# One set of buffers and PSUM banks for out projection, gate-up and down

## The chip, the cores and the metric

The kernel runs on one core of a Trainium2 chip. The metric is the device time of one launch in microseconds (us). The engines are TensorE (PE in the profile; PEld is its weight load), VectorE (DVE), ScalarE (ACT), GpSimd (POOL) and SyncE (SP), which here issues nearly all transfers. TensorE's clock has two levels, 1.2 and 2.4 GHz; the profile tells the granted share of the full one.

## What is computed

One layer of a latent model on 2048 tokens of width 1024: three parallel head groups (attention, a gated scan, Fourier mixing), an output projection, and a gated feed-forward network with 2816 hidden columns. The change concerns what follows the head groups:

```python
y = jnp.concatenate([attn, hg, fn], axis=-1) @ w_out[l]
x_new = x + g1 * y
x_new = x_new + g2 * swiglu_ffn(modulate(x_new, norm2_g[l], sh2, sc2), w_gate_up[l], w_down[l])
...
def swiglu_ffn(h, w_gu, w_dn):
    gate, up = jnp.split(h @ w_gu, 2, axis=-1)
    return (jax.nn.silu(gate) * up) @ w_dn
...
return rms_norm(x, final_norm_g)
```

All is float32.

## The kernel before

**Products.** Every float32 matrix product is made of three fp32r matmuls (`mm3`, lines 83 to 85): each operand is split into a high part (`hi`, line 72 on POOL, line 74 on ScalarE) and the rest (`lo`, line 79 on VectorE), and low x low is left out. So each operand tile costs a load, a cast and a subtraction before TensorE can use it.

**Out projection** (`project`, `second_norm`, `token_sums`; four blocks of 512 tokens). `mixed(b)` loads eight 128x512 tiles of the mixer's output from memory (`mr`, line 1118) and splits them to `hh` and `hl`; that of block 0 stands ahead of the last attention group, and the scheduler draws its work in among it. `project(b)` loads four 128x1024 row tiles of x (line 1130) and runs `rows_by_cols`: for each of two halves of 512 columns, two groups of four 128-row pieces of `w_out`, 1 MB a load (line 1044), split as a whole 128x2048 tile to `wh` and `wl`; 48 matmuls a group into four PSUM accumulators. `add_gated` (lines 1078 and 1079) adds g1 * y to x. `second_norm(b)` takes the mean squares on ScalarE (line 1086), stores the new rows to `xnew` (line 1140), scales them on POOL to `xn` (lines 124, 125, 1142), transposes them on TensorE in eight groups of four (line 1148), and ScalarE applies gain and shift to `xo` (line 1150), which is stored to `x2d` (line 1151). After the blocks 1 and 3 `token_sums` (lines 1158 to 1162) reads x2d back, forms four sums on VectorE (`block_sums`, lines 99 to 102) and stores them to `t2d`.

**Gate-up.** A seven-product (Winograd) scheme over a 2 x 2 split of tokens, depth and columns: `s` is one half of the tokens, and 22 units `j` of 128 hidden columns for each `s` take 44 units of seven products of twelve matmuls, in the order 6, 1, 5, 7, 2, 3, 4 and in three accumulators x, y, z. `operand(s, n)` (line 1201) loads the four tiles of product n's token operand through the slots `xraw` (four of them) and splits them to `xh`, `xl`. `fetch_w` (line 1213) loads a unit's weights, `left_sums` forms their sums (lines 94 to 97), `parts` splits them to `wp`. ScalarE, VectorE and POOL evacuate the accumulators (lines 1248 to 1273) to `e`, `f`, stored to `hid`.

**Down.** For each block `hidden(b)` loads and splits 22 tiles of `hid`, `rows_by_cols` multiplies them by `w_down` in groups of 1 MB, and `final` (lines 1097 to 1110) adds, normalises and stores.

**Order.** The three phases have pools of their own in SBUF and PSUM, opened and closed one after another, so a phase's first tiles wait for the end of the phase before where they take its space. Each engine runs its queue in order. The queues' order comes from a scheduler that moves instructions within what the data and the slots of the pools allow; SP's queue holds the transfers, and one that waits for a slot holds all behind it.

Of the kernel before, what the change touches and what calls it, by code (L numbers as in the profile page):

```python
# [42 lines left out]
def tile_backbone(  # L43
# [46 lines left out]
    def block_sums(x, o, left):  # L90

        x11, x12, x21, x22 = x
        if left:
            dve.tensor_tensor(o[0], x21, x22, ALU.add)
            dve.tensor_tensor(o[1], o[0], x11, ALU.subtract)
            dve.tensor_tensor(o[2], x12, o[1], ALU.subtract)
            dve.tensor_tensor(x21, x11, x21, ALU.subtract)
        else:
            dve.tensor_tensor(o[0], x12, x11, ALU.subtract)
            dve.tensor_tensor(o[1], x22, o[0], ALU.subtract)  # L100
            dve.tensor_tensor(o[2], x22, x12, ALU.subtract)
            dve.tensor_tensor(o[3], x21, o[1], ALU.subtract)
# [930 lines left out]

    with ExitStack() as ph:
        b2 = ph.enter_context(tc.tile_pool(name="p5b2", bufs=2, reuse_waits="tile"))
        hp = ph.enter_context(tc.tile_pool(name="p5h", bufs=13, reuse_waits="tile"))
        psd = ph.enter_context(tc.tile_pool(name="p5psd", bufs=4, side="right", reuse_waits="tile", space=PSUM))

        def split_w(loads, n):
            raw = b2.tile([P, 2048], F32, tag="wr", name="wr")  # L1040
            h = b2.tile([P, 2048], F32R, tag="wh5", name="wh5")
            l = b2.tile([P, 2048], F32R, tag="wl5", name="wl5")
            for dst, src in loads(raw):
                sp.dma_start(dst, src)
            hi(pool, h[:, :n], raw[:, :n])
            lo(l[:, :n], raw[:, :n], h[:, :n])
            return h, l

        def hidden_pair():
            return (hp.tile([P, TB], F32R, tag="hh", name="hh"),  # L1050
                    hp.tile([P, TB], F32R, tag="hl", name="hl"))

        def rows_by_cols(ah, al, w, kts, evac):

            last = len(kts) - 1
            for n in range(2):
                acc = [psd.tile([P, 512], F32, tag="dn", name="dn") for _ in range(4)]
                for i0 in range(0, len(kts), 4):
                    ni = min(4, len(kts) - i0)

                    def loads(raw):
                        return [(raw[:, :ni * 512].rearrange("p (k n) -> p k n", k=ni),
                                 w[kts[i0] * P:(kts[i0] + ni) * P, n * 512:(n + 1) * 512]
                                 .rearrange("(k p) n -> p k n", p=P))]
                    wh, wl = split_w(loads, ni * 512)
                    for t in range(4):
                        ts = slice(t * P, (t + 1) * P)
                        for i in range(ni):
                            ks = slice(i * 512, (i + 1) * 512)
                            mm3(acc[t], ah[i0 + i][:, ts], al[i0 + i][:, ts], wh[:, ks], wl[:, ks],  # L1070
                                i0 + i == 0, i0 + i == last)
                for t in range(4):
                    evac(t, n, acc[t])

        def add_gated(xs, gb):
            def evac(t, n, acc):
                ns = slice(n * 512, (n + 1) * 512)
                dve.tensor_tensor(acc, acc, gb[:, ns], ALU.mult)
                dve.tensor_tensor(xs[t][:, ns], acc, xs[t][:, ns], ALU.add)
            return evac  # L1080

        def mean_squares(xs):
            sq = b2.tile([P, 4], F32, tag="sq5", name="sq5")
            for t in range(4):
                junk = b1.tile([P, D], mybir.dt.bfloat16, tag="junk5", name="junk5")
                act.activation(junk, xs[t], AF.Square, accum_out=sq[:, t:t + 1])
            return rstd(b2, sq, 4, 1.0 / D, "r5")

        def final(b, xs):
            add = add_gated(xs, g2b)  # L1090
            sq = b2.tile([P, 4, 2], F32, tag="sq5f", name="sq5f")
            rs = b2.tile([P, 4, 2], F32, tag="rs5f", name="rs5f")

            def evac(t, n, acc):
                add(t, n, acc)
                junk = b1.tile([P, D], mybir.dt.bfloat16, tag="junk5", name="junk5f")
                act.activation(junk[:, :512], xs[t][:, n * 512:(n + 1) * 512], AF.Square, accum_out=sq[:, t, n:n + 1])
                if n == 0:
                    pool.tensor_scalar(rs[:, t, 0:1], sq[:, t, 0:1], 1.0 / D, EPS, ALU.mult, ALU.add)
                    return  # L1100
                pool.tensor_scalar(rs[:, t, 1:2], sq[:, t, 1:2], 1.0 / D, rs[:, t, 0:1], ALU.mult, ALU.add)  # L1101
                pool.tensor_tensor(rs[:, t, 0:1], rs[:, t, 1:2], half[:, 0:1], ALU.pow)  # L1102
                for s in range(2):
                    ns = slice(s * 512, (s + 1) * 512)
                    if s == 0:
                        dve.scalar_tensor_tensor(xs[t][:, ns], xs[t][:, ns], rs[:, t, 0:1], fgb[:, ns], ALU.mult, ALU.mult)
                    else:
                        act.activation(xs[t][:, ns], xs[t][:, ns], AF.Identity, scale=rs[:, t, 0:1])  # L1108
                        pool.tensor_tensor(xs[t][:, ns], xs[t][:, ns], fgb[:, ns], ALU.mult)  # L1109
                    sp.dma_start(out[0, b * TB + t * P:b * TB + (t + 1) * P, ns], xs[t][:, ns])  # L1110
            return evac

        def mixed(b):

            mh, ml = [], []
            for k in range(KT):
                raw = b2.tile([P, TB], F32, tag="mr", name="mr")
                sp.dma_start(raw, mixt[b][k * P:(k + 1) * P, :])
                h, l = hidden_pair()
                hi(act, h, raw)  # L1120
                lo(l, raw, h)
                mh.append(h)
                ml.append(l)
            return mh, ml

        def project(b, m):
            xs = []
            for t in range(4):
                xt = b1.tile([P, D], F32, tag="xt5", bufs=8, name="xt5")
                sp.dma_start(xt, x[0, b * TB + t * P:b * TB + (t + 1) * P, :])  # L1130
                xs.append(xt)
            rows_by_cols(m[0], m[1], w_out[0], list(range(KT)), add_gated(xs, g1b))
            return xs

        def second_norm(b, xs):

            r = mean_squares(xs)
            xn = []
            for t in range(4):
                sp.dma_start(xnew[b][t * P:(t + 1) * P, :], xs[t])  # L1140
# [227 lines left out]
```

## Time and profile before

| | |
|---|---|
| median of 3 runs | 3398.04 us (3397.04 to 3400.17) |
| profiled execution | 3395.07 us |
| its span | 3393.1 us |
| mean granted clock | 0.972 |
| TensorE busy | 3171.0 us (93%) |
| VectorE, ScalarE, POOL busy | 62%, 29%, 28% |

In the profiled execution the out projection's first matmul starts at 1754.9 us, gate-up's first at 2027.87, down's first at 2898.27, and the last matmul at 3379.4. In the timeline and groups, a line reads: line, engine, operation, written tile <- read tiles, shape, count; [idle before <- what ended it].

### The profile page before, as it was taken

Reading aid. Unit: us, or ns where it says so; the run is one execution under the profiler, and the core shown is the slowest. Engines: PE = TensorE matmul, PEld = TensorE weight load, DVE = VectorE, ACT = ScalarE, POOL = GpSimd, SP = SyncE. Lnnn points to the kernel's source line nnn. Section 1 sums busy time; section 2 is a strip of 40 time slices with the busy share of each in tenths; the row PEclk is TensorE's granted clock in tenths of the full one; section 3 lists DMA queues with packets and bytes.
Section 4 is the critical chain, followed back from the end, with each engine's and each line's share of the span. In section 5 each row is a group of like instructions: output and inputs, shape, how many; then the busy total and the mean of one; then the engine's idle time right before and its main releaser. Section 6 shows DMA issues by size and latency. Waiting matters only on the chain. (4 is left out here: it accounts for less than half of the span.)

```text
span 3393.1 us, 45128 instructions
## 1 busy us (share of the span) xinstructions
PE 3171.0 (93%) x17034; PEld 2648.8 (78%) x17034; DVE 2100.7 (62%) x3087; ACT 975.4 (29%) x2036; POOL 961.3 (28%) x1061
## 2 busy tenths in 40 slices
PE   7999999999889999999999849999999999899998
PEld 5777777787678888888887637888878887688886
DVE  6675665657776676776565447666776664554443
ACT  3222231222335555555542212111221111221110
POOL 3443444425411111110013213333233332232332
PEclk8999999999899999999999969999999999899999
DMA  6523232242541121221047764222432322664542
GB/s 225 170 70 123 76 115 83 61 133 67 169 136 51 35 63 51 76 61 35 7 145 249 264 211 142 80 89 75 137 106 77 91 75 71 231 210 152 181 157 79
DMA packets 355149, 392.49 MB, mean 116 GB/s; under 512 B 46362, under 2 KB 236660, under 8 KB 353908
## 3 DMA queue, kind: packets, MB, share of 16 engines
q1 hardware_dynamic: 340292, 378.59, 35.3%
q10 hardware_dynamic: 13776, 8.92, 0.8%
q8 instruction: 135, 2.21, 0.3%
q0 software_dynamic: 864, 2.10, 0.2%
q14 instruction: 82, 0.67, 0.1%
HBM read 302.77 MB, written 86.77 MB: 115 GB/s over the span
## 5 line engine op out<-in xcount | busy, mean ns | idle before, releaser
L83 PE MATMUL dn<-wl,hh 128*128 128x512 f32 x960 | 377.5, 393 | 20.4 <-DVE wl L79 20.4
L85 PE MATMUL dn<-wh,hl 128*128 128x512 f32 x960 | 377.1, 393 | 0.0
L84 PE MATMUL dn<-wh,hh 128*128 128x512 f32 x960 | 376.6, 392 | 0.0
L890 DVE TENSOR_REDUCE mx<-sc 128x1 f32<-128x512 f32 (+1 forms) x320 | 202.0, 632 | 122.3 <-PE sc L888 121.5
L72 POOL TENSOR_SCALAR wh<-wr 128x2048 fp32r<-128x2048 f32 x64 | 119.5, 1868 | 482.4 <-PE dn L85 388.0
L83 PE MATMUL y<-xl,wp 128*128 128x512 f32 x528 | 207.2, 393 | 45.9 <-DVE xl L79 42.3
L79 DVE TENSOR_TENSOR wp<-wr,wp 128x512 fp32r<-128x512 f32 x176 | 167.8, 954 | 120.6 <-POOL wp L72 117.8
L79 DVE TENSOR_TENSOR ptl<-ptv,pth 128x512 fp32r<-128x512 f32 x288 | 196.4, 687 | 67.1 <-ACT pth L74 64.7
L74 ACT CAST pth<-ptv 128x512 fp32r<-128x512 f32 x288 | 169.6, 593 | 236.2 <-PE ptv L904 228.6
L79 DVE TENSOR_TENSOR wl<-wr,wh 128x2048 fp32r<-128x2048 f32 x64 | 139.4, 2178 | 151.2 <-POOL wh L72 147.3
L896 ACT ACTIVATE p<-sc,mx 128x512 f32<-128x512 f32 (+1 forms) x320 | 201.9, 649 | 91.7 <-DVE mx L893 87.8
L83 PEld LDWEIGHTS dn<-wl,hh 128*128 128x128 f32 x960 | 181.2, 189 | 59.9 <-issue 20.6
L72 POOL TENSOR_SCALAR wp<-wr 128x512 fp32r<-128x512 f32 x176 | 132.3, 752 | 290.3 <-PE x L85 167.0
L85 PEld LDWEIGHTS dn<-wh,hl 128*128 128x128 f32 x960 | 181.1, 189 | 39.1
L84 PEld LDWEIGHTS dn<-wh,hh 128*128 128x128 f32 x960 | 181.1, 189 | 38.6
L84 PE MATMUL y<-xh,wp 128*128 128x512 f32 x528 | 206.9, 392 | 0.0
L85 PE MATMUL y<-xh,wp 128*128 128x512 f32 x528 | 206.4, 392 | 0.0
L888 PE MATMUL sc<-kth,q 128*128 128x512 f32 (+1 forms) x640 | 194.8, 378 | 0.0
L85 PE MATMUL accf<-xh,wl 128*128 128x512 f32 x448 | 184.6, 412 | 10.2 <-DVE wl L79 10.2
L79 DVE TENSOR_TENSOR wl<-wraw,wh 128x1536 fp32r<-128x1536 f32 (+3 forms) x78 | 118.5, 1519 | 119.6 <-POOL wh L72 117.7
L888 PE MATMUL sc<-kp,q 128*128 128x512 f32 (+1 forms) x640 | 190.0, 373 | 0.0
L79 DVE TENSOR_TENSOR hl<-mr,hh 128x512 fp32r<-128x512 f32 x120 | 98.3, 831 | 140.7 <-ACT hh L74 136.4
(350 smaller groups left out, 8067.4 us busy)
## 6 DMA issues: line engine op xcount, KB each, us to landing
wr<-in_w_gate_up_dram SPq DMA_DIRECT2D x88, 512.0 KB, 5.1
wr<-in_w_down_dram SPq DMA_DIRECT2D x40, 1024.0 KB, 5.1
wraw<-in_w_in_dram SPq DMA_DIRECT2D x112, 256.0 KB, 3.8
mr<-hid SPq DMA_DIRECT2D x88, 256.0 KB, 3.3
xt<-in_x_dram SPq DMA_DIRECT2D x32, 512.0 KB, 6.2
wm<-in_w_mod_dram SPq DMA_DIRECT2D x64, 256.0 KB, 2.8
wr<-in_w_out_dram SPq DMA_DIRECT2D x16, 1024.0 KB, 6.4
hid<-f SPq DMA_DIRECT2D x44, 256.0 KB, 3.8
```

The costliest lines, as they stand in the source:

```text
L72: pool.tensor_scalar(dst, src, 1.0, 0.0, ALU.mult, ALU.add)
L74: act.copy(dst, src)
L79: (eng or dve).tensor_tensor(dst, src, h, ALU.subtract)
L83: pe.matmul(ps, ah, bl, start=first, stop=False, skip_group_check=more)
L84: pe.matmul(ps, ah, bh, start=False, stop=False, skip_group_check=more)
L85: pe.matmul(ps, al, bh, start=False, stop=last, skip_group_check=more)
L888: pe.matmul(s[:, :n], a[:, ts], bb[:, js], start=i == 0, stop=i == 4)
L890: dve.tensor_reduce(mx[:, j:j + 1], s[:, :n], AX.X, ALU.max)
L896: act.activation(u["p"][:, a:e], u["s"][i][:, :e - a], AF.Exp, bias=mx[:, 5:6], accum_out=mx[:, 6 + i:7 + i])
```

## The change

Out projection, gate-up and down get one set of pools. Raw weights, raw mixer tiles and raw token sums share two slots of 128x4x512 (`raw4`). Split weights of all phases are 128x2x512 tiles of `wp`, nine of them (POOL casts one 512-wide part, VectorE subtracts). Operand pairs sit in 28 slots (`h1` to `h7`, `l1` to `l7`, four each); x rows borrow pairs 4 and 5. PSUM is handed out by `bank` from two pools of four in turn. The `xraw` slots fall from four to two (three in down). Loads of x and stores of xnew are 512 columns wide (256 KB) and the row scaling is in place.

Order in the program: a group's weights are loaded and split one group ahead (`Groups.ahead`). The transposes of block b - 1 (`turn_rows`) stand between the two halves of `project(b)`; those of block 3 in gate-up's unit 0. The sums of the first token half are formed on POOL during blocks 2 and 3 (`early_sums`), three of four stored and the fourth split at once as operand 6; those of the second half on VectorE in units 2 to 5 of gate-up. Operands 1, 7, 5 and the first unit's weights are loaded in block 3; operands 2, 3, 4 in unit 0. Down's first weights and 12 hidden tiles are split in the last unit. The matmuls and transposes are as many as before.

```diff
+        wr = ph.enter_context(tc.tile_pool(name="p5w", bufs=2, reuse_waits="tile"))
+        wp = ph.enter_context(tc.tile_pool(name="p5p", bufs=9, reuse_waits="tile"))
+        xa = ph.enter_context(tc.tile_pool(name="p5xa", bufs=4, reuse_waits="tile"))
+        psa = ph.enter_context(tc.tile_pool(name="p5psa", bufs=4, side="right", reuse_waits="tile", space=PSUM))
...
+        def bank(name):
+            banks["n"] += 1
+            return (psa, psb)[(banks["n"] - 1) // 4 % 2].tile([P, TB], F32, tag="bank", name=name)
...
+        def raw4(name):
+            return wr.tile([P, 4, TB], F32, tag="wr", name=name)
+
+        def wparts(src):
+            w = wp.tile([P, 2, TB], F32R, tag="wp", name="wp")
+            hi(pool, w[:, 0, :], src)
+            lo(w[:, 1, :], src, w[:, 0, :])
+            return w
...
+            def ahead(self, i):
+                if i < len(self.specs) and i not in self.done:
+                    self.done.add(i)
+                    self.load(i)
+                    for k in range(4):
+                        self.split(i, k)
+                self.load(i + 1)
...
+        st = gs.enter_context(tc.tile_pool(name="p5s", bufs=2, reuse_waits="tile"))
...
+            for g in range(2):
+                i = b * 4 + c * 2 + g
+                if i + 1 < len(wo.specs):
+                    wo.ahead(i + 1)
+                else:
+                    first_unit(0, 5)
+                w = wo.parts.pop(i)
+                for t in range(4):
+                    rows(acc[t], t, m, w, 4 * g, 4, KT)
...
+        def token_sums(s, k, eng):
+
+            raw = raw4("xr")
+            for i in range(4):
+                sp.dma_start(raw[:, i, :], x2d[s][i][k * P:(k + 1) * P, :])
+            t = st.tile([P, 3, TB], F32, tag="ws", name="ts")
+            block_sums(eng, [raw[:, i, :] for i in range(4)], [t[:, 0, :], t[:, 1, :]], False)
+            return raw[:, 0, :], (t[:, 0, :], t[:, 1, :], raw[:, 1, :], raw[:, 2, :])
...
-                raw = st.tile([P, TB], F32, tag="xraw", bufs=4, name="xraw")
+                raw = st.tile([P, TB], F32, tag="xraw", name="xraw")
...
+        def early_sums(ks):
+            for k in ks:
+                b11, ts = token_sums(0, k, pool)
+                keep_sums(0, k, ts, (0, 2, 3))
+                xo.setdefault(6, []).append(split(6, "xo", ts[1]))
+
+        wo.ahead(0)
+        xs = load_rows(0)
+        for b in range(NB):
+            sq = st.tile([P, 2, 4], F32, tag="sq5", name="sq5")
+            project(b, 0, m, xs, sq)
+            if b > 0:
+                turn_rows(b - 1, before)
+            if b + 1 < NB:
+                nm = mixed(b + 1)
+                nx = load_rows(b + 1)
+                if b + 2 == NB:
+                    early_sums((0, 1))
+            else:
+                wo.ahead(len(wo.specs) - 1)
+                xo |= {n: operand(0, n) for n in (1, 7, 5)}
+                raws.extend([fetch_w(0), fetch_w(1)])
+                raws.append(left_sums(raws.pop(0)))
+            project(b, 1, m, xs, sq)
+            scale_rows(xs, sq)
+            if b + 2 == NB:
+                early_sums((2, 3))
...
+                if i == 0 and n == 7:
+                    turn_rows(NB - 1, before)
+                if i == 0 and n == 1:
+                    xo |= {q: operand(0, q) for q in (2, 3, 4)}
...
+                elif o < 3:
+                    more_hidden(4 * (o + 1))
+                    if o == 0:
+                        wd.load(0)
+                        wd.load(1)
+                    for k in ((0, 1), (2,), (3,))[o]:
+                        wd.split(0, k)
+                    wd.done.add(0)
+            if s == 0 and 2 <= j < 6:
+                b11, ts = token_sums(1, j - 2, dve)
+                keep_sums(1, j - 2, ts, range(4))
```

The order of the engines' queues, where it moves, at three places. ScalarE at the end of attention, before the change (`pth` and `rbc` belong to attention, `hh` is the cast of block 0's mixer tiles):

```order
L74 CAST pth<-ptv 128x512
L74 CAST hh<-mr 128x512 x2
L74 CAST pth<-ptv 128x512 x3
L923 COPY rbc<-ptrc 128x512
L74 CAST pth<-ptv 128x512 x2
L74 CAST hh<-mr 128x512 x2
```

The same place in the changed kernel, where `mxh` is the cast of the mixer tiles:

```order
L74 CAST pth<-ptv 128x512
L74 CAST mxh<-mr 128x512 x8
L74 CAST pth<-ptv 128x512 x3
L923 COPY rbc<-ptrc 128x512
L74 CAST pth<-ptv 128x512 x5
L937 COPY at<-ptvu 128x512
```

All eight casts of the mixer's tiles now stand in one piece, ahead of the last attention casts. The next place is POOL in the out projection from block 2 to block 3, before (`wh` are the high parts of w_out, `xn` the scaled rows of block 2):

```order
L72 TENSOR_SCALAR wh_18001<-wr 128x2048
L72 TENSOR_SCALAR wh_18055<-wr 128x2048
L124 TENSOR_SCALAR r5m<-sq_18164 128x4
L125 TENSOR_TENSOR r5r<-r5m,half 128x4
L1142 TENSOR_SCALAR xn_18178<-xt_17868,r5r 128x1024
```

And after (`ts` and `xr` are the token sums, `xs` the rows scaled in place, `ss` the mean squares of block 2):

```order
L72 TENSOR_SCALAR wp<-wr 128x512 x8
L99 TENSOR_TENSOR ts<-xr 128x512
L100 TENSOR_TENSOR ts<-xr,ts 128x512
L101 TENSOR_TENSOR xr<-xr 128x512
L102 TENSOR_TENSOR xr<-xr,ts 128x512
...
L124 TENSOR_SCALAR r5m<-ss_18308 128x4
L125 TENSOR_TENSOR r5r<-r5m,half 128x4
L1160 TENSOR_SCALAR xs<-xs,r5r 128x512 x5
L72 TENSOR_SCALAR wp<-wr 128x512 x4
```

Two sets of four sums, which VectorE did before, stand ahead of the scaling of block 2 and of the split of block 3's first weights. The third place is SP's queue there, after (`xr` are the loads for the sums, `t2d` their stores, `wr_18176` block 3's first piece of w_out):

```order
L1177 DMA xr_18126<-x2d03_96 128x512
L1177 DMA xr_18143<-x2d00_93 128x512
L1184 DMA t2d00_101<-ts_18131 128x512
L1177 DMA xr_18143<-x2d01_94 128x512
L1177 DMA xr_18143<-x2d02_95 128x512
L1184 DMA t2d02_103<-xr_18126 128x512
L1184 DMA t2d03_104<-xr_18126 128x512
L1177 DMA xr_18143<-x2d03_96 128x512
L1184 DMA t2d00_101<-ts_18148 128x512
L1152 DMA xnew2_91<-xs_17687 128x512
L1079 DMA wr_18176<-in_w_out_dram 128x4x512
```

The piece of w_out, before alone among the stores of the transposed rows, now comes behind the loads and stores of the sums, and takes one of the two slots that these use.

## Rows read from the trace of the kernel before

**Rows 1.** Stretches: length, busy time (instructions) by engine, clock, DMA share, GB/s.

```profile
1800.00:1850.00 50.00, 47.10 (x212) 37.76 (x211) 24.88 (x25) 13.53 (x22) 15.76 (x10) 0.97 0.71 235
1850.00:1900.00 50.00, 46.69 (x209) 37.26 (x208) 25.53 (x32) 13.21 (x22) 13.54 (x9) 0.97 0.83 288
...
2000.00:2050.00 50.00, 20.94 (x74) 15.19 (x75) 37.06 (x52) 11.91 (x20) 12.90 (x15) 0.67 0.79 252
2050.00:2450.00 400.00, 399.78 (x1763) 330.20 (x1762) 277.85 (x377) 75.26 (x126) 130.11 (x168) 1.00 0.32 96
...
2927.00:3380.00 453.00, 452.75 (x1998) 374.56 (x1996) 198.23 (x188) 73.15 (x141) 126.54 (x99) 1.00 0.47 156
```

**Rows 2.** TensorE's waits after 1750 us: total us, times, longest.

```profile
PE y L83 <- DVE xl L79: 42.3, 1, 42.3
PE pt L1148 <- POOL xn L1142: 20.1, 7, 8.2
...
PE dn L83 <- DVE wl L79: 20.2, 1, 20.2
PE y L83 <- DVE t L1262: 3.6, 1, 3.6
```

**Rows 3.** TensorE's paces: one stretch, then timeline rows (start, busy us).

```profile
1768.00:1804.00 36.00, 36.00 (x156) 29.02 (x155) 25.25 (x28) 9.19 (x16) 7.66 (x5) 1.00 0.85 301
...
2028.43 0.63 PE L84 MATMUL y<-xh,wp 128*128 128x512 f32 x1
2028.86 0.63 PE L85 MATMUL y<-xh,wp 128*128 128x512 f32 x1
...
1917.23 5.53 PE L1148 MATMUL pt<-ident,xn 128*128 128x128 f32 x25 [0.20 <-POOL xn L1142]
```

**Rows 4.** Groups: line, engine, operation, count | busy us, mean ns | idle before.

```profile
L83 PE MATMUL dn<-wl,hh 128*128 128x512 f32 x960 | 377.5, 393 | 20.4 <-DVE wl L79 20.4
...
L72 POOL TENSOR_SCALAR wp<-wr 128x512 fp32r<-128x512 f32 x176 | 132.3, 752 | 290.3 <-PE x L85 167.0 <-issue 79.7 <-PE z L85 39.5
...
L1256 POOL TENSOR_TENSOR e<-e,e 128x512 f32<-128x512 f32 x44 | 57.4, 1306 | 11.3 <-ACT e L1255 11.3
...
L1150 ACT ACTIVATE xo<-pt,mod2t,gain 128x512 f32<-128x512 f32 x32 | 23.3, 776 | 40.6 <-PE pt L1148 26.5 <-DMA x2d<-xo 13.9
```

**Rows 5.** Timeline: first matmul of the out projection, last one of down.

```profile
1754.93 0.40 PE L83 MATMUL dn<-wl,hh 128*128 128x512 f32 x1
...
3379.36 0.39 PE L85 MATMUL dn<-wh,hl 128*128 128x512 f32 x1
```

**Rows 6.** Timeline of ScalarE at the end of attention.

```profile
1742.14 1.17 ACT L74 CAST hh<-mr 128x512 fp32r<-128x512 f32 x2
```

**Rows 7.** Transfers: count, KB each, median us from issue to landing.

```profile
wr<-in_w_out_dram SPq DMA_DIRECT2D x16, 1024.0 KB, 6.4
...
x2d<-xo SPq DMA_DIRECT2D x32, 256.0 KB, 4.2
xr<-x2d SPq DMA_DIRECT2D x32, 256.0 KB, 4.6
t2d<-xs SPq DMA_DIRECT2D x32, 256.0 KB, 3.0
```

**Rows 8.** A stretch of 10 us in the out projection, columns as in rows 1.

```profile
1830.00:1840.00 10.00, 10.00 (x45) 8.05 (x44) 4.00 (x4) 0.00 (x0) 1.91 (x1) 1.00 1.00 371
```

**Rows 9.** Timeline of POOL and VectorE with splits side by side.

```profile
2000.11 1.04 POOL L72 TENSOR_SCALAR wp<-wr 128x512 fp32r<-128x512 f32 x1
...
2000.59 1.09 DVE L79 TENSOR_TENSOR wp<-ws,wp 128x512 fp32r<-128x512 f32 x1
```

**Rows 10.** The raw operand tiles: duration ns min/median/max; time to landing.

```profile
L74 ACT CAST xh<-xraw x56: 606/621/628, 1989.0 to 2472.4; 128x512 fp32r<-128x512 f32 x56
L79 DVE TENSOR_TENSOR xl<-xraw,xh x56: 674/684/1137, 2027.0 to 2474.2; 128x512 fp32r<-128x512 f32 x56
...
DMA to landing us min/median/max: 2.5/3.2/5.1
```

More of the change, by code (lines that the diff above doesn't have):

```diff
@@ L1053, in rows_by_cols @@
[L1053 to L1111, printed above, removed]
@@ L1113, in mixed @@
-        def mixed(b):
[L1115 to L1133, printed above, removed]
@@ new lines, in rows @@
+        def rows(acc, t, m, w, k0, nk, kts):
+            ts = slice(t * P, (t + 1) * P)
+            for i in range(nk):
+                mm3(acc, m[k0 + i][0][:, ts], m[k0 + i][1][:, ts], w[i][:, 0, :], w[i][:, 1, :], k0 + i == 0, k0 + i == kts - 1)
+        def mixed(b):
+            out = []
+            for n, k0 in zip((1, 7) if b % 2 == 0 else (2, 3), (0, 4)):
+                raw = raw4("mr")
+                sp.dma_start(raw, mixt[b][k0 * P:(k0 + 4) * P, :].rearrange("(k p) n -> p k n", p=P))
+                out += [split(n, "mx", raw[:, k, :]) for k in range(4)]
+            return out
@@ L1164, in tile_backbone @@
         m = mixed(0)
+        wo = Groups(w_out[0], [(n, k0, 4) for _ in range(NB) for n in range(2) for k0 in (0, 4)])
         tasks = []
@@ new lines, in tile_backbone, with more_hidden @@
+        blocks6 = raws.pop()
+        DG = [(k0, min(4, HT - k0)) for k0 in range(0, HT, 4)]
+        wd = Groups(w_down[0], [(n, k0, nk) for _ in range(NB) for n in range(2) for k0, nk in DG])
+        hidden = []
+        stage = {}
+        def more_hidden(upto):
+            while len(hidden) < min(upto, NB * HT):
+                i = len(hidden)
+                raw = stage["p"].tile([P, TB], F32, tag="xraw", name="hr")
+                sp.dma_start(raw, hid[i // HT][i % HT * P:(i % HT + 1) * P, :])
+                hidden.append(split(ORDER[i // 4 % 7], "hd", raw))
@@ L1248, in tile_backbone @@
                     act.copy(e6, acc)
-                    if i + 1 < len(units):
+                    if not end:
                         blocks6 = left_sums(raws.pop(0))
@@ new lines, in tile_backbone @@
+                if not end:
+                    nxt[n] = wparts(blocks6[n])
+                elif o < 3:
[9 more added lines that the diff above has]
+                keep_sums(1, j - 2, ts, range(4))
```

250 lines of the change are left out of this document (133 added, 117 removed).

## The prediction

> **What bounds the kernel now.** I read the table of stretches first [rows 1]. From 2050 to 2450 us and from 2927 to 3380 us TensorE is busy all the time, at full granted clock: gate-up and down stand at TensorE's own pace, and no better order can gain there. The 50 us stretches of the out projection and of the step into gate-up are another picture: TensorE is busy for 47 of 50 us in two of them and for 20.94 in the last, at a granted clock of 0.67. The list of TensorE's waits names what ended these gaps [rows 2]: 42.3 us for the first operand of gate-up, 20.1 us in seven waits of the second norm's transposes for POOL's scaling, 20.2 us for down's first weights, 3.6 us where the operands are exchanged between the two token halves. That is 86.2 us.
>
> How much is lost in all? Two paces say it. In down, 1998 matmuls take 452.75 us, 0.2266 us each [rows 1]; in an undisturbed piece of the out projection 156 take 36 us, 0.231 us [rows 3]. After a gap the clock is at its lower level and a matmul starts every 0.43 us [rows 3] (its second and third row). The work is 960 x 3 = 2880 matmuls in the two projections [rows 4] and 44 units of 84 in gate-up, 6576 together: 1490 us at 0.2266. 768 of them belong to the out projection, + 3 us. The 128 transposes cost about 0.1 us each (an estimate: a run of 25 took 5.53 us at a lowered clock, the last of [rows 3]), 13 us. Sum 1506 us. From 1754.9, where the out projection's first matmul stands, to the last at 3379.6 [rows 5] the trace has 1624.7 us, an estimated 4 us of it for the last attention matmuls. **The loss is about 114 us**: 86 us of gaps, the rest slow clock after them and shorter waits. This is all that the change can win; it removes no matmul.
>
> **The change, part by part.** It does not take the causes of the gaps away, it puts their work earlier, beside TensorE's work. Each of the old gaps goes: the first unit's operands and weights are split during the last half of the out projection, the transposes of a block stand between the halves of the next, and down's first weights and 12 hidden splits stand in the last gate-up unit. So I strike the 114 us and ask what is late next, term by term, along the order of the changed kernel.
>
> *End of attention.* ScalarE now has eight mixer splits ahead of the last attention casts, before two; VectorE has their eight second halves and the first weight splits. Two casts take 1.17 us [rows 6], so six more cost 3.5 us on ScalarE, and VectorE about as much again in the same chain. I take 6 us, from 3 (VectorE's share hidden) to 9 (the weight splits in front too).
>
> *Join of blocks 2 and 3.* Let T be the start of the second half of block 2. The last transposed tile of the first token half leaves ScalarE 8 x 0.776 = 6 us later [rows 4] and lands after 4.2 us [rows 7], T + 11 with the queue; the load for the sums takes 4.6 us (T + 16); four sums on POOL at 1.306 us take 5.2 (T + 21) [rows 4]; their store takes 3.0 (T + 24). Only then is the shared raw slot free for block 3's first w_out load, which takes 6.4 us (T + 31), and its first split, 0.752 us on POOL [rows 4] and some 1.09 on VectorE [rows 9], makes T + 33. TensorE's 96 matmuls of the half end at T + 22 to 24. So it waits about 10 us, and 2 more for the clock. The order has the load behind the sums on SP's queue, and four more sums stand ahead of the row scaling on POOL. DMA is nearly full there: block traffic drove its share to 1.00 at 371 GB/s in one stretch of 10 us [rows 8]. I take 15 us, from 4 (the scheduler's loads land sooner) to 24 (every transfer at half speed).
>
> What VectorE and POOL do to each other is in [rows 9]: of two splits side by side POOL's takes 1.04 us and VectorE's 1.09, more than POOL's mean of 0.752 [rows 4] and VectorE's median of 0.684 [rows 10]. So each stretches the other, and the chain above has VectorE's stretched value. The Trainium skill ("SBUF — State Buffer", section "SBUF: two separate sides") says that a VectorE operation with two SBUF inputs and a GpSimd operation that reads SBUF lock the shared port pair, and the loser waits for the whole instruction. By that each of the four sums on the chain could wait a further 0.68 us, + 2.7 us, and the forecast would be 3337. The trace agrees only in part: its pair shows both engines busy from 2000.59 to 2001.15.
>
> *Unit 0.* The scale of block 3 stands behind ScalarE's evacuations, and three operands are loaded inside the unit: 6 us, from 1 to 15.
>
> *Exchange of the operands between the token halves.* The raw slots fall from four to two. A load takes 3.2 us, the cast 0.62, VectorE's part 0.68 [rows 10], with about 0.4 to issue: 4.9 us for a slot, with two slots 2.45 for each of 28 splits, 68.6 us. In the changed order 249 matmuls stand between the first and the last of them, 56.4 us. So 12 us are uncovered; before, with four slots, 3.6. I take 13 us with the clock, from 6 (loads at their minimum of 2.5 us) to 25 (at 5.1 for half of them).
>
> *Waits at the transposes.* They now stand between matmuls that are ready, so 1.5 us, from 0 to 5.
>
> *The rest*: the second w_out load of block 3, the start of down, the gate sums. Down's hidden splits are ready about 10, 20 and 32 us after the last unit's first product and needed at 19, 30 and 41, so that start is covered; if that cover fails, the 20.2 us of before come back. The chain behind the last matmul is the same code. 8 us, from 3 to 12.
>
> *At nothing*: splitting w_out in four parts of 512 columns takes POOL 0.752 x 4 = 3 us for a group [rows 4] and VectorE 4 x 1.09 at most; the 48 matmuls of a group, 11 us, cover both, and TensorE would pay what goes beyond 11. Smaller x and xnew transfers are twice as many on SP's queue; a half block's 6.3 million bytes take 17 us at the rate of [rows 8], beside 22 us of matmuls, and what they cost without that cover is B's price below.
>
> Sum of new losses: 6 + 15 + 6 + 13 + 1.5 + 8 = 49.5 us. Gain 114 - 49.5 = 64.5 us. The profiled execution took 3395.07 us; the median of the three runs is 3398.04, 3 us above it. 3398.0 - 64.5 = **3334 us** (rounded). The ends of the terms sum to 17 and 90, which would be 3301 and 3374, but they will not all fall one way.
>
> **The rivals.** *A: as above*, 3315 to 3350, chance 0.50.
>
> *B: the out projection becomes a DMA stage.* Each block moves w_out 4 MB, mixer 2, x 2, xnew 2, transposed rows 2, 12.6 million bytes; with the sums (7.3), the operands (3.1) and two gate weights the new order packs 63 MB into about 206 us, 306 GB/s, which no 50 us stretch of before reached: its four full stretches of the out projection moved 261.5 on average, from 235 to 288 [rows 1]. At that mean 63 MB take 241 us, 35 more: **3369 us**. Against it: at share 1.00 the engines moved 371 GB/s [rows 8], so the mean of before is what its gaps asked for, not a limit. Chance 0.22. The Trainium skill ("DMA: Bandwidth & Descriptors", section "Specifications") gives a core about 358 GB/s of HBM; by it 63 MB want 176 us, which is under 206. The trace's 371 is slightly above that figure.
>
> *C: the joins are covered.* If the loads at the join land before they are wanted and the exchange hides behind its 56 us, only the smaller terms stay, about 20 us: 3398 - 94 = **3304 us**. For it: two transfers that land in 3 us take most of the join's wait away. Against it: the join's chain above adds up with no slack. Chance 0.16.
>
> *D, slower: two raw slots act as one.* If the next load goes out only when the split before it is through, a split costs c = 4.9 us instead of 2.45. The 28 splits of the exchange and 22 of the first operands have 56 + 63 us of TensorE work beside them, so the loss is 50c - 119, with 30 us for the other terms. It eats the whole 114 us at c = 4.06; at 4.9 the loss is 156 us, 42 us slower: **3440 us**. For it: every such load waits on SP's one queue, where a wait holds all that follows. Against it: with four slots the exchange left only 3.6 us uncovered [rows 2], which a chain of 28 x 4.9 = 137 us could not have done. Chance 0.07.
>
> *E: nothing changes.* The order may be all that moves, with the clock's loss kept at the new joins; between C, B and D, 3391 to 3405. Chance 0.05.
>
> **How the numbers follow.** Faster and slower are counted beyond 0.2% (7 us), about what a measurement of this kernel can tell from no change. Faster: A, C and nearly all of B, 0.87. Same: E and the top of B, 0.05. Slower: D and a part of B joined to a late down start, 0.08. The range has to leave out 0.2: D, E and the top of B (0.14) above, and the part of C below 3298 (0.05). That gives 3298 to 3382 around 3334.
>
> **What would show it.** Right: no wait of TensorE above 5 us between the last attention matmul and block 2; one wait near the join of blocks 2 and 3, about 10 us, for a weight part; no 42 us gap before gate-up and no 20 us gap before down; granted clock over 0.9 in each 50 us stretch of the out projection; some 10 us around the exchange, ended by operand splits. The step on the join is wrong if the wait before block 3's first half is under 4 us; the step on the slots if 28 splits follow each other at 1.3 us. B is shown by a DMA share of 0.95 or more through two blocks with waits for transfers at each of them; D by operand loads that each start after the split before; the prediction as a whole is wrong if a wait over 25 us stands anywhere, above all at down's start.

## The result, and the profile after

The changed kernel takes **3349.06 us** (median of 4 runs, 3348.41 to 3351.47) against 3397.54 us for the kernel before on the same chip: a ratio of 0.9861, 95% interval 0.9849 to 0.9873. It is 1.4% faster. The forecast was 3334 us: the direction holds, the size was 15 us too good. In the profiled executions the span goes from 3393.1 to 3346.7 us.

TensorE's waits after 1735 us, in the changed kernel (what waited <- what ended it: total us, times, longest):

```profile
PE pt L1167 <- POOL xs L1160: 14.6, 4, 10.2
PE pt L1167 <- DVE xs L1149: 10.0, 6, 2.3
PE z L83 <- DVE xol L79: 9.2, 9, 1.6
PE ptv L904 <- DVE ptl L79: 7.3, 3, 4.0
PE y L83 <- DVE xol L79: 2.1, 4, 0.8
```

Set against [rows 2]: the 42.3 us before gate-up and the 20.2 us before down are gone. What is left are short waits, and the largest is one of 10.2 us. The stretches that hold them (length, busy time and instructions by engine, granted clock, DMA share, GB/s, as in [rows 1]):

```profile
1829.70:1840.30 10.60, 5.47 (x35) 4.49 (x34) 7.29 (x12) 6.51 (x14) 0.20 (x1) 0.75 0.48 165
...
1894.20:1917.30 23.10, 23.09 (x98) 18.67 (x96) 9.04 (x13) 9.20 (x19) 5.29 (x4) 0.95 0.92 319
1917.30:1957.50 40.20, 29.27 (x128) 23.48 (x128) 18.59 (x22) 9.39 (x19) 33.09 (x34) 0.83 0.77 254
1980.10:2050.00 69.90, 60.27 (x243) 46.11 (x243) 54.18 (x75) 26.39 (x45) 31.11 (x36) 0.90 0.56 172
2425.00:2480.00 55.00, 47.34 (x182) 34.30 (x181) 38.55 (x55) 17.73 (x30) 14.11 (x17) 0.94 0.56 165
...
2850.00:2900.00 50.00, 50.00 (x223) 41.40 (x222) 27.82 (x42) 15.17 (x25) 13.03 (x19) 1.00 0.70 237
```

The first is the transposes of block 0, the second and third the second half of block 2 and the join behind it, then gate-up's first units, the exchange of the operands, and the step into down, whose first matmul stands at 2854.43: TensorE works through it without a gap. The loss of a stretch is its length less its matmuls at 0.2266 us and its transposes at 0.1 us (a row's count holds one more, which reaches in over its start): 10.6 - 2 x 0.2266 - 3.2 = 6.9 us for the first; 69.9 - 210 x 0.2266 - 3.2 = 19 us for gate-up's start; 55 - 181 x 0.2266 = 14 us for the exchange.

### The profile page after: what moved, and what is told of

It is laid out like the page before. It is cut to its first block, busy times and chain, and to the rows that moved or that the text cites. A ratio compares the mean times of both kernels' runs of the same rounds, so it can differ in the third digit from the quotient of the medians.

```text
span 3346.7 us, 45666 instructions
## 1 busy us (share of the span) xinstructions
PE 3172.7 (95%) x17034; PEld 2653.5 (79%) x17034; DVE 2154.6 (64%) x3251; ACT 974.6 (29%) x2068; POOL 1057.7 (32%) x1269
## 5 line engine op out<-in xcount | busy, mean ns | idle before, releaser
L84 PE MATMUL dn<-wp,hdh 128*128 128x512 f32 x704 | 273.9, 389 | 0.0
L83 PE MATMUL dn<-wp,hdh 128*128 128x512 f32 x704 | 273.9, 389 | 0.0
L85 PE MATMUL dn<-wp,hdl 128*128 128x512 f32 x704 | 273.9, 389 | 0.0
L79 DVE TENSOR_TENSOR wp<-wg,wp 128x512 fp32r<-128x512 f32 x176 | 172.3, 979 | 100.4 <-POOL wp L72 97.9
L83 PE MATMUL y<-xol,wp 128*128 128x512 f32 x528 | 207.5, 394 | 2.3 <-DVE xol L79 2.1
L72 POOL TENSOR_SCALAR wp<-wg 128x512 fp32r<-128x512 f32 x176 | 125.5, 713 | 258.3 <-PE x L85 134.3
L84 PE MATMUL y<-xoh,wp 128*128 128x512 f32 x528 | 206.7, 391 | 0.0
L85 PE MATMUL y<-xoh,wp 128*128 128x512 f32 x528 | 206.3, 392 | 0.0
L72 POOL TENSOR_SCALAR wp<-ws 128x512 fp32r<-128x512 f32 x132 | 100.2, 759 | 296.8 <-PE y L85 158.8
L904 PE MATMUL ptv<-ident,p 128*128 128x128 f32 x1152 | 180.1, 276 | 9.1 <-DVE ptl L79 7.7
L83 PE MATMUL accf<-xl,wh 128*128 128x512 f32 x448 | 183.3, 409 | 0.0
L84 PE MATMUL accf<-xh,wh 128*128 128x512 f32 x448 | 182.1, 407 | 0.0
```

The lines of the kernel that those rows point to most:

```text
L72: pool.tensor_scalar(dst, src, 1.0, 0.0, ALU.mult, ALU.add)
L79: (eng or dve).tensor_tensor(dst, src, h, ALU.subtract)
L83: pe.matmul(ps, ah, bl, start=first, stop=False, skip_group_check=more)
L84: pe.matmul(ps, ah, bh, start=False, stop=False, skip_group_check=more)
L85: pe.matmul(ps, al, bh, start=False, stop=last, skip_group_check=more)
L904: pe.transpose(pt[:, i, u * P:(u + 1) * P], ps[u]["p"][:, (2 * g + i) * P:(2 * g + i + 1) * P], ident)
```

## The experiments

Each is an edit of the changed kernel unless it says otherwise. Ratios are to the kernel before, which ran beside each; a difference to the changed kernel is the difference of the ratios times 3397.5 us, and with intervals of about 0.0015 either way one of less than some 7 us is not clear of the noise. Then the trace alone speaks. For that the last column takes the profiled execution: the time from the first matmul behind attention's last one to the last matmul of down, against 1565.3 us in the changed kernel. It leaves out the head groups, whose instructions the runs have in common and whose end varies from 1762.7 to 1770.2 us.

| | median us | ratio (95% interval) | against the changed kernel | the same in the trace, behind attention |
|---|---|---|---|---|
| e1_banks | 3346.57 | 0.9855 (0.984 to 0.987) | -2 us | -1.6 us |
| e2_slots1 | 3425.3 | 1.0086 (1.0071 to 1.0101) | +76 us | +79.9 us |
| e3_slots3 | 3335.5 | 0.9824 (0.9809 to 0.9839) | -13 us | -8.6 us |
| e4_sums_dve | 3344.26 | 0.9844 (0.9827 to 0.986) | -6 us | +1.6 us |
| e5_turn_split | 3337.19 | 0.9834 (0.9817 to 0.985) | -9 us | -12.4 us |
| e6_no_down | 3345.95 | 0.9863 (0.9846 to 0.988) | +1 us | +4.5 us |
| e7_late_first | 3349.99 | 0.987 (0.9855 to 0.9885) | +3 us | -1.5 us |
| e8_turn_slots3 | 3326.89 | 0.9805 (0.979 to 0.9819) | -19 us | -17.3 us |
| e9_own_pools | 3348.31 | 0.9867 (0.9851 to 0.9884) | +2 us | +2.6 us |
| e10_all3 | 3328.07 | 0.9805 (0.9791 to 0.982) | -19 us | -19.7 us |
| e11_late_sums | 3330.69 | 0.9808 (0.9793 to 0.9822) | -18 us | -20.1 us |
| e12_moved_pools | 3358.72 | 0.9897 (0.9881 to 0.9914) | +12 us | +12.5 us |

**The transposes of blocks 0 and 1.** This term was one of the two furthest off. The changed kernel's TensorE there (start, busy us, [idle before <- what ended it]):

```profile
1829.71 2.35 PE L1167 MATMUL pt<-ident,xs 128*128 128x128 f32 x20
1833.55 0.66 PE L1167 MATMUL pt<-ident,xs 128*128 128x128 f32 x4 [1.49 <-DVE xs L1149]
1836.55 1.11 PE L1167 MATMUL pt<-ident,xs 128*128 128x128 f32 x4 [2.35 <-DVE xs L1149]
1838.95 1.11 PE L1167 MATMUL pt<-ident,xs 128*128 128x128 f32 x4 [1.28 <-DVE xs L1149]
```

Five groups of four run at once, the last three wait each for line 1149, which is VectorE's gating add of the block whose half has just been multiplied. That add reads no transposed row. It frees a PSUM bank. Theory: eight groups need eight banks, four of which hold the accumulators just finished.

e1_banks:

```diff
+            if name in ("op", "pt5"):
+                return (psa if name == "op" else psb).tile([P, TB], F32, tag="bank", name=name)
```

> Edit: the accumulators of the out projection always take the first four PSUM banks, the transposes always the second four; nothing else is written differently. Theory (the transposes of blocks 0 and 1 wait for VectorE's evacuation of the accumulators because eight transposed groups need banks that the accumulators just held): TensorE's waits at the transposes that end with the gating add on VectorE, 10.0 us in the changed kernel, are gone; about 1 to 3 us per block of waits for ScalarE's evacuation of the transposed groups take their place, since four banks must serve eight groups; time about 3342 us, from 3338 to 3347. Rival (the transposes wait for their data or for the scaling, and the name of the wait is a coincidence): the 10 us stay and the time is 3349 us.

The waits changed their name, as the theory says, and not their size:

```profile
PE pt L1169 <- POOL xs L1162: 14.4, 3, 8.8
PE pt L1169 <- ACT xo L1171: 9.8, 2, 5.2
```

No wait on VectorE's add is left at a transpose; ScalarE's evacuation of the transposed groups has taken its place, 9.8 us for 10.0. I had put that at 1 to 3 us a block and it was 5. So four banks for eight groups are too few, whoever frees them.

e5_turn_split has in addition:

```diff
-                turn_rows(b - 1, before)
+                turn_rows(b - 1, before, (0, 1, 4, 5))
...
             project(b, 1, m, xs, sq)
+            if b > 0:
+                turn_rows(b - 1, before, (2, 3, 6, 7))
```

> Edit: as in e1_banks, and four of a block's eight transposed groups stand after the first half of the next block, the other four after its second half, so that each time four banks are enough. Theory (banks set the loss at the transposes): the waits of 10 us on VectorE's or ScalarE's evacuations are gone, blocks 0 and 1 lose under 3 us in place of 14; the join keeps a wait of some 10 us, since the sums now start half a block later for part of the data; time about 3338 us, from 3332 to 3346. Rival (the loss at the transposes is their own time and the clock, wherever they stand): 3347 us or more.

3337.19 us, where 3338 was expected. Waits on evacuations at the transposes fall to 0.9 us in all:

```profile
PE op L83 <- DVE wp L79: 12.4, 3, 8.0
...
PE pt L1169 <- ACT xo L1171: 0.9, 1, 0.9
```

The first row holds the join: its longest wait now stands in front of block 3's first matmul, for a weight part, and the other two stand inside block 3. The banks are the cause of the loss at the transposes: with four groups for four banks blocks 0 and 1 lose 2 us in all, the clock behind the transposes included.

**The raw operand slots.** e2_slots1 and e3_slots3 change one number:

```diff
-                raw = st.tile([P, TB], F32, tag="xraw", name="xraw")
+                raw = st.tile([P, TB], F32, tag="xraw", bufs=1, name="xraw")
```

(bufs=3 in e3_slots3, and the same for the hidden tiles of the last unit.)

> Edit: one raw operand slot in place of two (gate-up's operands and the hidden tiles split in its last unit). Theory (each slot is held for load, cast and subtraction, 4.9 us by the prediction; the pace of the splits is that over the number of slots): the casts follow each other at about 4.9 us in place of 2.4; the 28 splits of the exchange take 137 us beside 56 us of matmuls, so the loss there grows from 14 to about 80 us; the first operands lose about 40 us more; time about 3450 us, from 3420 to 3490, slower than the kernel before. Rival (the splits are paced by SP's queue or by ScalarE, not by the slots): the time grows by less than 30 us.

> Edit: three raw operand slots in place of two. Theory (the pace is the slot's hold over the number of slots): casts at about 1.6 us; 28 of them take 46 us beside 56 us of matmuls, so the loss of 14 us around the exchange falls to about 3, and unit 0's loss of 19 us falls by some 8 (the rest is the late scaling of block 3's rows); time about 3330 us, from 3324 to 3338. Rival (the waits come from transfers held in SP's queue behind stores): less than 6 us gained.

ScalarE's casts of the exchange with one slot, then in the changed kernel with two, then with three:

```profile
2501.51 0.62 ACT L74 CAST xoh<-xraw 128x512 fp32r<-128x512 f32 x1 [3.34 <-DMA xraw<-t2d]
2505.44 0.62 ACT L74 CAST xoh<-xraw 128x512 fp32r<-128x512 f32 x1 [3.32 <-DMA xraw<-x2d]
```

```profile
2429.11 0.62 ACT L74 CAST xoh<-xraw 128x512 fp32r<-128x512 f32 x1 [1.70 <-DMA xraw<-t2d]
2431.05 0.62 ACT L74 CAST xoh<-xraw 128x512 fp32r<-128x512 f32 x1 [0.84 <-DMA xraw<-t2d]
2433.61 0.62 ACT L74 CAST xoh<-xraw 128x512 fp32r<-128x512 f32 x1 [1.45 <-DMA xraw<-t2d]
```

```profile
2434.87 0.62 ACT L74 CAST xoh<-xraw 128x512 fp32r<-128x512 f32 x1 [1.27 <-DMA xraw<-x2d]
2436.20 0.62 ACT L74 CAST xoh<-xraw 128x512 fp32r<-128x512 f32 x1 [0.70 <-DMA xraw<-x2d]
```

Each waits for its transfer. From the first to the last of the 28 casts the mean step is 4.50 us with one slot (2434.7 to 2556.2), 2.57 with two (2403.2 to 2472.7) and 1.72 with three (2397.3 to 2443.7). Step times slots is 4.5, 5.1 and 5.2: the hold of a slot divided by the slots, as the prediction had it (4.9). With one slot the kernel is slower than before, 3425 us where about 3450 was expected: the exchange lost 55 us and not 80. With three it gains 13 us by the medians and 8.6 in the trace, 6 of them around the exchange (its loss goes from 14 to 8) and 3 at the step into gate-up. Inside unit 0 the loss falls from 19 to 13, but a new wait of 2.8 us for a weight part stands ahead of it. I had expected 11 and 8, so the slots are the smaller part of unit 0's loss.

**The join of blocks 2 and 3.** In the changed kernel, T (the start of block 2's second half) is 1894.1. POOL, with the sums and the scaling, then SP's load of block 3's weights, then TensorE (timeline rows):

```profile
1911.94 1.29 POOL L99 TENSOR_TENSOR ts<-xr 128x512 f32<-128x512 f32 x1 [27.41 <-DMA xr<-x2d]
1913.30 1.30 POOL L100 TENSOR_TENSOR ts<-xr,ts 128x512 f32<-128x512 f32 x1
1914.56 1.29 POOL L101 TENSOR_TENSOR xr<-xr 128x512 f32<-128x512 f32 x1
1915.81 1.74 POOL L102 TENSOR_TENSOR xr<-xr,ts 128x512 f32<-128x512 f32 x1
...
1926.72 3.36 POOL L1160 TENSOR_SCALAR xs<-xs,r5r 128x512 f32<-128x512 f32 x5
1930.05 3.24 POOL L72 TENSOR_SCALAR wp<-wr 128x512 fp32r<-128x512 f32 x4
```

```profile
1919.69 0.45 SPq L1079 DMA_DIRECT2D wr<-in_w_out_dram  x1
```

```profile
1927.47 1.15 PE L1167 MATMUL pt<-ident,xs 128*128 128x128 f32 x3 [10.18 <-POOL xs L1160]
```

The sums start at T + 18 (forecast T + 16), the load goes out at T + 25.6 (T + 24), its split begins at T + 36. The half's matmuls end at 1917.3, and from there to block 3's first matmul at 1931.9 are 14.6 us, 1.6 of them for 16 transposes. What the list of waits names is another thing than the forecast: the scheduler drew block 2's transposes ahead of block 3, and they wait for the row scaling, which stands behind eight sums on POOL.

> Edit: the token sums of the first token half are formed on VectorE in place of POOL. Theory (the 10.2 us wait of block 2's transposes is POOL's queue: the row scaling stands behind eight sums of 1.3 us): the wait falls to about 3 us, the loss at the join from 14 to about 6, the time to about 3341 us, from 3338 to 3345. Rival (the sums wait for their loads, and POOL's share is hidden; or VectorE's evacuations are late in turn): the join's wait stays above 8 us and the time within 3 us of 3349.

The edit is one word (`dve` for `pool` in `early_sums`). The join's wait went from 10.2 to 7.2 us:

```profile
PE pt L1167 <- POOL xs L1160: 13.3, 5, 7.2
```

The time is 6 us less, which the interval does not quite part from none, and the trace has no gain behind attention (+1.6 us): gate-up's first matmul stands 216.7 us behind the end of attention, in the changed kernel 212.6. POOL's queue is a part of the wait, 3 us of it, and not all, and the 3 us were lost again before gate-up. e8_turn_slots3 joins e5_turn_split and e3_slots3, e10_all3 adds the sums on VectorE, e11_late_sums puts these half a block later:

```diff
-                if b + 2 == NB:
-                    early_sums((0, 1))
             else:
+                early_sums((2, 3))
...
             if b + 2 == NB:
-                early_sums((2, 3))
+                early_sums((0, 1))
```

> Edit: e5_turn_split and three raw operand slots together. If the two causes are apart (banks in blocks 0 and 1, slots in unit 0 and the exchange) their gains add: 13.5 us measured for the slots and what e5_turn_split gains, about 3326 us. If they share a cause, the sum falls short by more than 5 us.

> Edit: e8_turn_slots3, and the first half's token sums on VectorE. If the join's wait is the chain of sums, stores and block 3's weight load that the prediction describes, four sums of 0.7 in place of 1.3 us shorten it by 2.4 us a round, and the scaling stands behind no sums on POOL: 5 us gained by e4_sums_dve would come again, about 3322 us. Rival (with the transposes split the load's slot alone decides, not the sums): within 2 us of 3327.

> Edit: e10_all3 with the sums written half a block later: those of the first two row groups after block 2's second half, the other two within block 3, so that block 3's first two weight loads no longer wait for the sums' raw slots. Theory (the join's wait of 8 to 13 us is block 3's weight load waiting for a slot that the sums hold): no wait over 3 us before block 3's first matmul; some of it may come back before gate-up, as the sums now lie nearer to it; time about 3315 us, from 3310 to 3324. Rival (the load is late because DMA is full, or the chain is only moved): time as e10_all3 or more, with a wait of over 8 us in block 3 or before gate-up.

e8_turn_slots3 is the fastest by median of all kernels here, **3326.89 us, ratio 0.9805**. Its 19 us are 3 short of the 9 + 13 of its parts, less than the 5 that would have told of a shared cause and less than the noise, so the banks and the slots pass for separate causes. e10_all3 gained nothing more by the median: once the transposes are split, the wait of 9 us stands at the weight load, and the rival of its expectation holds. In e11_late_sums that wait is gone. TensorE at block 3's first matmul, in e10_all3 and then in e11_late_sums:

```profile
1915.57 0.79 PE L83 MATMUL op<-wp,mxh 128*128 128x512 f32 x1 [9.22 <-DVE wp L79]
```

```profile
1901.54 0.50 PE L83 MATMUL op<-wp,mxh 128*128 128x512 f32 x1 [1.66 <-DVE xs L1151]
```

So the sums' hold on the slot is what kept block 3's weights late, as the theory has it, and gate-up's first matmul stands 8.6 us earlier behind attention than in e10_all3. But 4.7 us are still waited inside block 3, 5.8 us came before gate-up, as the sums now lie there, and gate-up's first units lost 19 us where e10_all3 lost 11:

```profile
PE y L83 <- POOL wp L72: 5.8, 1, 5.8
...
PE op L83 <- DVE wp L79: 4.7, 1, 4.7
```

Behind attention the two kernels differ by 0.4 us in all, and the medians by 3 us the other way (the trace of e11_late_sums is that of its fastest execution, 3323.51 us). The join's work was moved, not hidden.

**Why the gaps before gate-up and down went.** e6_no_down takes the early splits out of the last unit, e7_late_first writes operands 1, 7, 5 and the first unit's weights behind the out projection:

```diff
-                elif o < 3:
-                    more_hidden(4 * (o + 1))
-                    if o == 0:
-                        wd.load(0)
-                        wd.load(1)
...
+        wd.ahead(0)
         for b in range(NB):
```

```diff
-                else:
-                    first_unit(0, 5)
...
+        xo |= {n: operand(0, n) for n in (1, 7, 5)}
+        raws.extend([fetch_w(0), fetch_w(1)])
+        raws.append(left_sums(raws.pop(0)))
+        first_unit(0, 7)
         blocks6 = raws.pop()
```

> Edit: the lines that split down's first weights and twelve hidden tiles in the last gate-up unit are taken out; the same work is written after the last unit. Theory (what removed the 20 us gap before down is the written place): a gap of 15 to 20 us comes back before down's first matmul, time about 3367 us. Rival (the shared buffers and banks alone let the scheduler draw this work into the last unit): no gap over 3 us, time 3349 us.

> Edit: the first unit's operands 1, 7, 5, its weights' loads and its weight splits are written after the out projection in place of inside its last half. Theory (the written place removes the 42 us gap): loads and splits follow the last half block, a loss of some 30 us more than in the changed kernel, time about 3380 us. Rival (with shared slots the scheduler draws them in by itself): within 6 us of 3349.

My theory fell in both. Neither time moved beyond the noise (+1 and +3 us; the +4.5 in e6_no_down's trace are of its slowest execution, with a wait of 12.1 us at the join), and e6_no_down has no wait of TensorE in down at all: the scheduler draws this work into the phase before by itself, wherever it is written. So something else let it. e9_own_pools is e6_no_down with pools of down's own, opened after the others are closed:

```diff
         gs.close()
+        ph.close()
+        wr = ph.enter_context(tc.tile_pool(name="p7w", bufs=2, reuse_waits="tile"))
+        wp = ph.enter_context(tc.tile_pool(name="p7p", bufs=9, reuse_waits="tile"))
...
```

> Edit: as e6_no_down (down's first work written after gate-up), and the buffers and banks of down are pools of its own, as many and as large, opened after the others are closed. Theory (sharing the pools is what lets the scheduler draw down's first work into the last unit): with pools of its own the weight splits and most hidden splits come after the last unit's end again, and a gap of 8 to 20 us stands before down's first matmul, time 3357 to 3370 us. Rival (the gap went for another reason, such as splits of 512 columns in place of 2048): no gap over 4 us, time 3346 to 3351 us.

This fell too: 3348.31 us, and the only wait in down is

```profile
PE dn L83 <- DVE wp L79: 1.9, 2, 1.5
```

But by their sizes and their order these pools lie on the same memory as the shared ones, raw weights on raw weights. In e12_moved_pools they are opened as xb, xa, the PSUM pools, wp, wr, and nothing else differs:

> Edit: e9_own_pools with down's pools opened in another order, operands first and raw weights last, so that down's raw weights lie where gate-up's last operands and evacuation buffers lay, which are in use to the end of the last unit, instead of where its raw weights lay, which are free half a unit before. Nothing else. Theory (what a buffer lies on decides how early its load can go; the gap of 20 us before was a weight load that waited for memory in use up to the last products): the weight loads move behind the last unit's stores on SP's queue and a gap of 6 to 15 us stands before down's first matmul, time 3355 to 3366 us. Rival (the gap of before came from the loads of x rows and hidden tiles that stood ahead of the weights, or from 2048-wide splits, and where buffers lie does not matter): no gap over 3 us, time 3346 to 3351 us.

3358.72 us, 12 us more than the changed kernel and 10 more than e9_own_pools, with a gap at down's start (SP in e9_own_pools, then SP, POOL and TensorE in e12_moved_pools):

```profile
2828.09 0.93 SPq L1079 DMA_DIRECT2D wr<-in_w_down_dram  x2
```

```profile
2856.10 0.32 SPq L1308 DMA_DIRECT2D hid<-f  x1
2856.67 0.38 SPq L1079 DMA_DIRECT2D wr<-in_w_down_dram  x1
```

```profile
2862.24 3.23 POOL L72 TENSOR_SCALAR wp<-wr 128x512 fp32r<-128x512 f32 x4 [17.24 <-DMA wr<-in_w_down_dram]
```

```profile
PE dn L83 <- DVE wp L79: 7.5, 1, 7.5
PE dn L83 <- ACT hdh L74: 1.3, 1, 1.3
PE dn L85 <- DVE hdl L79: 1.2, 2, 1.0
```

The first weight load goes out behind a store of the last unit, at 2856.67 in place of 2828.09, and TensorE waits for its split. What the new buffers lie on decides here how early the first load of the phase can go. That gives 10 us of waits; the 20.2 us of [rows 2] had further parts, such as the row tiles and hidden tiles loaded ahead of the weights, which no run here took apart.

For the 42.3 us before gate-up the runs tried only the written place of the loads and splits, and the trace of the kernel before points at something else. ScalarE casts the first operand at 1989.0, and VectorE subtracts it only at 2027.0 [rows 10]. VectorE's queue between them ends so:

```profile
2024.07 0.69 DVE L99 TENSOR_TENSOR xs<-xr 128x512 f32<-128x512 f32 x1 [6.43 <-DMA xr<-x2d]
...
2026.44 0.68 DVE L102 TENSOR_TENSOR xs<-xr,xs 128x512 f32<-128x512 f32 x1
2027.04 2.49 DVE L79 TENSOR_TENSOR xl<-xraw,xh 128x512 fp32r<-128x512 f32 x4
```

All four sets of token sums of the second half stand ahead of the first operand, from 1987.03 on, and wait for their loads. The change moves these sums into units 2 to 5 of gate-up; they run there from 2059 to 2124 us, in e7_late_first too. That move is the likely reason why the gap went. No run put the sums back, so it is not shown.

## Why the prediction was right or wrong

*The loss of 114 us, and that the change can win no more*: right as a frame. The profiled span fell by 46.4 us, so new losses of about 68 us took the place of the old, where the sum had 49.5. Three readings behind the 114 are off, by some 2 us together: the out projection's first matmul stands at 1749.95 and not at 1754.9, with six of them ahead of that time; attention's matmuls behind 1754.9 take 2.2 us and not 4; and a matmul of the out projection starts every 0.2333 us and not 0.231, as the 156 of [rows 3] hold two that reach over the ends. And there was something more to win: the out projection's matmuls became faster, 5 us in all (last section), which nobody forecast.

*End of attention, 6 us*: right. The last attention matmul comes 6.7 us later, with eight out-projection matmuls (1.8 us) fewer done by then; the trace was already 2.2 us late at 1703, before the moved casts. 6.3 us.

*Join, 15 us*: right in size, 13 us and about 1 of slow clock, and in the times of its chain within 2 us up to the load. The split, forecast at T + 31, began at T + 36. Wrong in what stands in front: the scaling behind the sums and not the weight load alone. With the transposes split the load is what TensorE waits for, 9 us, as forecast, and with the sums out of its way 1.7.

On the locked port the Trainium skill ("SBUF — State Buffer", section "Who interferes with whom") says that a VectorE instruction with two SBUF inputs contends with a GpSimd instruction that reads SBUF, and one with at most one SBUF input, outside its 2-port modes, does not. The rows of the join agree in direction: the sum at 1915.81 took 1.74 us in place of 1.29 while VectorE subtracted two SBUF tiles (1915.29, 1.11 us), and the sum at 1911.94 kept its 1.29 beside a VectorE multiply that reads PSUM:

```profile
1911.89 0.70 DVE L1148 TENSOR_TENSOR op<-op,g1b 128x512 f32<-128x512 f32 x1 [1.29 <-PE op L85]
...
1915.29 1.11 DVE L79 TENSOR_TENSOR xol<-ts,xoh 128x512 fp32r<-128x512 f32 x1
```

The delay was 0.45 us, less than the 0.68 that I had worked out.

*Exchange, 13 us*: right, 14 us; the step of 2.57 us was forecast as 2.45, and the runs with one and three slots show that the slot's hold sets it.

*Transposes, 1.5 us*: **the first step that failed.** "They now stand between matmuls that are ready" looked at data and forgot the PSUM banks. Blocks 0 and 1 lost 6.9 and 6.6 us there, and about 1 us each at the lowered clock behind them; e1_banks and e5_turn_split show why. That is 14 us more than the 1.5.

*Unit 0, 6 us with a bound of 15*: **the second**, mis-sized, 19 us. The scaling of block 3 on POOL alone held TensorE for 4.2 us; operand splits, most at 2.4 to 3 us a step, made nearly all other waits, and the granted clock was 0.90. Three slots took 6 us off and put a wait of 2.8 ahead; the rest was not taken apart.

*The rest, 8 us*: too much. Down's start lost nothing; the other half of block 2's transposes, inside block 3, some 2 us. The out projection's matmuls were quicker than the 0.231 us assumed, 3 us in all. The sum of what was measured, with the join's slow clock, that behind the transposes and the 2.2 us at 1703: 6 + 13 + 1 + 14 + 13.5 + 2 + 19 + 2 - 3 + 2 = 69.5, within 2 us of the 68.

*That the work's new place removes the old gaps*: the gaps went, but the written place of the loads and splits is not what removed them (e6_no_down, e7_late_first). Before down the memory is a part of it (e12_moved_pools); before gate-up it is most likely the place of the second half's sums, which the prediction does not name, and the cause stays open.

*The signs.* No wait over 5 us ahead of block 2, one of about 10 at the join (for scaled rows and not for a weight part), and no old gap: these came. The granted clock over 0.9 in each 50 us of the out projection did not: from 1900 to 1950 it was 0.86, in the kernel before 0.90.

*The rivals.* A held by 1 us: 3349 in 3315 to 3350. B did not come: from 1894 to 1917 the DMA share was 0.92 at 319 GB/s with TensorE busy all the time; it never held two blocks. C needed the join covered, and it was not. D's mechanism is real and only its condition was not met: with a slot less the step is 4.5 us, for which its formula gives 50 x 4.5 - 119 + 30 = 136 us of loss, 3420 us, and 3425 was measured. The near hit is in part luck, as two terms of it were off: the exchange lost 55 us where the formula has 70, and gate-up's first units 48 where it has 36.

## What to carry to other kernels

When operations are moved between others, count the PSUM banks at the new place as well as the data: eight groups that follow four full accumulators wait for whoever evacuates them. With one to three slots the pace of the load-and-split chain was the hold of one slot divided by the slots, and the hold could be read from the trace of before. Where a scheduler orders the work, the memory that a phase's first buffers lie on can matter more than the place where the code is written, as at down's start: put the buffers that are loaded first on memory that falls free first. And before a gap is put down to a late load, look at what stands ahead in the queue of the engine that ended the wait: there it was sums that nothing needed yet.

## What was not expected of the hardware

The same 128x512 matmuls of the out projection start every 0.2333 us in the kernel before (153 steps from 1768.14 to 1803.84, the stretch of [rows 3]) and every 0.2267 us in the changed one (274 from 1767.58 to 1829.71), both at full granted clock. The share of DMA is not the cause. A stretch of the kernel before and one of the changed kernel (columns as in [rows 1]):

```profile
1940.00:1950.00 10.00, 10.00 (x45) 8.01 (x44) 6.53 (x10) 0.00 (x0) 1.93 (x1) 1.00 0.01 2
```

```profile
1900.00:1910.00 10.00, 10.00 (x46) 8.29 (x45) 2.17 (x4) 2.13 (x4) 0.00 (x0) 1.00 0.99 318
```

With next to no transfers the step in the first is 0.2333 us, and at a share of 0.99 it is 0.2267 in the second. What else differs, such as the shape of the weight tiles, no run took apart, so the cause stays open.
